# Group 0's experts on one shared tile of tokens, its rows gathered on TensorE

## The chip, the cores and the metric

One of the eight cores of one Trainium2 chip runs the whole kernel. The metric is device microseconds of one execution, lower is better. The engines are TensorE (PE; PEld is its weight load), VectorE (DVE), ScalarE (ACT), GpSimd (POOL) and SyncE (SP), which only issues DMAs here. Each engine has a queue of its own and works in program order.

## The reference

One decoder layer on 512 tokens of 1024 channels, in float32: `x1 = x + gate1 * mixer(h)`, then a hierarchical mixture of experts on `h2 = rms_norm(x1) * g + sh`, where `g` and `sh` are rows made from the condition `c`.

```
grp = softmax(h2 @ w_group + b_group); g = argmax(grp)             # one of 4 groups per token
sel = (h2 @ w_router + b_router) of group g; top 2 of its 4 experts
y   = sum over the 2 experts of  p_g * softmax(top 2) * (silu(h2 @ w_gate) * (h2 @ w_up)) @ w_down
out = x1 + gate2 * y
```

There are 16 experts in 4 groups; each has 3 MB of weights (1024x256 gate and up, 256x1024 down).

## The kernel before

The mixer runs first (to about 598 us), with `x1` as its result in two buffers, T1 (token tiles 0 and 1) and T2 (tiles 2 and 3) of 128 tokens each. Its last stage, the output projection, goes through steps (t, g) of token tile t and 256 columns g; (2,2), (2,3), (3,2), (3,3) are the last. `Weave` runs generators beside it: at each tick, those that are due emit their next piece, so the order on every engine is fixed when the program is built. `tile_chain(t)` takes the norm, logits and h2 rows of a finished tile; `h2_rows` writes the rows to a DRAM tile `h2_d`.

After (3,3) the last columns are transposed, `norm2(3)`, logits and `route(2)` give each token its group and experts, `ranks` (products with a triangular matrix) give every token its place among an expert's tokens, `one_hot(e)` makes a 128-column one-hot of the places, `slot_rows(e)` turns it into token numbers and POOL gathers the rows of `h2_d`. `busy(n)` are dummy products that keep TensorE occupied meanwhile.

The loop over `e` from 0 to 16 then works on 128 slots of one expert a turn: `gate_up` (in four parts), `act_t` (transposes the activation of the expert before), `x_rows(e + 1)` (eight transposes of gathered rows), `down(e - 1)`, with the next expert's weight splits and slots in between. Experts 0 to 3 are those of group 0, each with a tile of its own; then come eight of the two larger groups, the fullest of them a second time (index 7, by `EX`); the lightest of groups 1 to 3 shares one tile (`GL`, indices 13 to 16): one gather, one scatter, and `down` adds the four up in PSUM. `down` of a tile's last expert ends in a scatter with add to `out`. Experts with over 128 tokens besides go through a dynamic loop at the end.

Weights come as half-megabyte chunks through a ring of `NRAW` raw buffers (22), loaded by SP in an order `SEQ`; chunk j + NRAW takes the buffer of chunk j. Chunk numbers of expert e < 5: gate/up first half (0: 0, 1; 1: 2, 3; 2: 8, 9; 3: 14, 15; 4: 22, 23), down (0: 6, 7; 1: 12, 13; 2: 18, 19; 3: 24, 25). Chunks 16 and 17 use buffer T1, 18 and 19 use T2. Loads from chunk 26 on wait until chunk j - 5 has landed (`HOLD_FROM`, `AHEAD`). A new tile in a buffer waits until every access of the old tile, wherever it stands in the program, is done. A product of two float32 operands is exact enough as one native product or as three products of high and low halves (`mm3`, after `split` on ScalarE and VectorE); expert 0 is native, the second half of every gate/up too.

Of the kernel before, what the change touches and what calls it, by code (L numbers as in the profile page):

```python
# [171 lines left out]
def trunk(ctx: ExitStack, tc: tile.TileContext, I, out, dbg=None):  # L172
# [793 lines left out]
    def mod_rows(hf):  # L966
# [18 lines left out]
        for j in range(4):  # L985
# [14 lines left out]
            if hf == (j < 2):  # L1000
                A.dma_start(mod_d[1 - hf:2 - hf, 512 * (j % 2):512 * (j % 2) + 512], bm[0:1])
            yield 1

    def router_consts():
        lst = sml("lst")[:, 0:128]
        A.dma_start(lst, I["cst"][:, C_LST:C_END])
        A.dma_start(R.mcol, mod_d.rearrange("a (k p) -> p a k", p=128))
# [9 lines left out]
        V.scalar_tensor_tensor(R.mcol[:, 0], R.mcol[:, 0], 1.0, pv[:, PV_G2:PV_G2 + 8], OP.add, OP.mult)  # L1017
# [104 lines left out]
    NRAW = 2 * len(RAWS) + 2  # L1122
# [15 lines left out]
    held = []  # L1138

    def load_raw(j, hold=False, eng=SY):  # L1140
        if j >= 96:
            return
        if hold:
            held.append(j)
            return
# [6 lines left out]
        if j >= NRAW:  # L1152
            raws[j] = raws[j - NRAW]
            if j % 2 == 0:
                duo[j] = duo[j - NRAW]
        elif j % 2:
            raws[j] = raws[j - 1, 1]
        else:
            k = RAWS[j // 2] if j < 2 * len(RAWS) else "P"
            t = {"X": lambda: R.rawx.tile([128, 2048], FT, name="raw_x"),  # L1160
                 "P": lambda: R.ep.tile([128, 2048], FT, name="raw_p", bufs=1)}.get(k, lambda: big(k, "raw_e"))()
            raws[j], raws[j, 1] = t[:, 0:1024], t[:, 1024:2048]
            duo[j] = t
# [19 lines left out]
    def f():  # L1183
# [5 lines left out]
        for n, shp, dt in (("cst", [C_LST], FT), ("wrs", [8, 27], FT), ("brb", [27], FT), ("ex_i", [1], I32), ("ssp", [4, 4], FT), ("ssum", [4], FT),  # L1189
                           ("rs2", [4], FT), ("LG", [4, 27], FT), ("EL", [4, 22], FT), ("MT", [2, 4, 8], FT),   # L1190
                           ("mem", [4, 20], FR), ("lst", [128], FR), ("tok", [4, 4], FR), ("e16", [4, 16], FT), ("e4", [4, 4], FT), ("z", [2, 4], FT), ("nmem", [4, 20], FT), ("mcol", [2, 8], FT), ("PC", [20, 10], FT), ("PP", [8, 10], FT), ("PL", [4, 10], FT),
# [9 lines left out]
        R.xg = pool("xgp", wps).tile([128, 1024], FT, name="xg")  # L1201
# [31 lines left out]
    def logits(t, ks, last=7, b=None):  # L1233
# [17 lines left out]
    def norm_lg(t):  # L1251
        V.scalar_tensor_tensor(R.LG[:, t], R.LG[:, t], R.rs2[:, t:t + 1], R.brb, OP.mult, OP.add)

    def h2_gain(t, c0, n):
        c = slice(c0, c0 + n)
        G.tensor_tensor(R.xg[:, c], X1(t)[:, c], st["mod", 1][:, c], OP.mult)

    def h2_rows(t, hf, mode):
        s = slice(hf * 512, hf * 512 + 512)
        s2 = slice(1024 + hf * 512, 1024 + hf * 512 + 512)  # L1260
        h2 = sml("h2")
        rs, sh = R.rs2[:, t:t + 1], st["mod", 0][:, s2]
        if mode[0] == "V":
            V.scalar_tensor_tensor(h2, X1(t)[:, s], rs, st["mod", 1][:, s], OP.mult, OP.mult)
        elif mode == "A":
            A.activation(h2, X1(t)[:, s], AF.Copy, scale=rs)
            G.tensor_tensor(h2, h2, st["mod", 1][:, s], OP.mult)
        elif mode == "gA":
            A.activation(h2, R.xg[:, s], AF.Copy, scale=rs)
        if mode == "gV":  # L1270
            V.scalar_tensor_tensor(h2, R.xg[:, s], rs, sh, OP.mult, OP.add)
        else:

            def end(eng=G):
                eng.tensor_tensor(h2, h2, sh, OP.add)
                SY.dma_start(h2_d[t * 128:(t + 1) * 128, s], h2)
            if mode == "VV":
                return lambda: end(V)
            end()
            return  # L1280
        SY.dma_start(h2_d[t * 128:(t + 1) * 128, s], h2)
# [4 lines left out]
    def route(t0):  # L1286
# [3 lines left out]
        V.tensor_reduce(m1[:, :, 0:1], lg[:, :, 0:4], AX.X, OP.max)  # L1290
# [32 lines left out]
    def tile_chain(t):  # L1323
# [5 lines left out]
        logits(t, range(4, 8))  # L1329
        norm_lg(t)  # L1330
        if t == 1:
            route(0)
        yield 1
        h2_rows(t, 1, "A" if t < 1 else "V")
        if t < 2:
            h2_rows(t, 0, "V")
        else:
            st["h2"] = h2_rows(t, 0, "VV")

    def last_half():  # L1340
        x1_t(3, 512, 256)
        h2_gain(3, 512, 256)
        yield 1
# [21 lines left out]
    def f():  # L1365
# [3 lines left out]
        for t, g in seq:  # L1369
# [27 lines left out]
    def busy(n):  # L1397
        for _ in range(n):
            T.matmul(wb, ones_c, ones_c[:, None, :].to_broadcast([128, 4, 128]), start=True, stop=True)

    wb = bank("mm")
    lb = logits(3, (4, 5))
    busy(3)
# [5 lines left out]
    gp = pool("gp", es, bufs=5)  # L1409
# [9 lines left out]
    def w_units(w):  # L1419
# [5 lines left out]
        def gu_unit(q, i):  # L1425
# [11 lines left out]
            if q % 2:  # L1437
                load_raw(AT[w, j] + NRAW, hold="placed" not in st)
# [12 lines left out]
    def used(e):  # L1451
# [21 lines left out]
    def slot_rows(e, b=None):  # L1473
# [4 lines left out]
        idx = R.sm2.tile([128, 1], I32, name="idx", bufs=8)  # L1478
        V.tensor_copy(idx, b[:, 0:1])
        X = st["mod", 1][:, 0:1024] if e % 2 else ep.tile([128, 1024], FT, name="X", bufs=1)  # L1480
        G.indirect_dma_start(X, None, h2_d, bass.IndirectOffsetOnAxis(idx[:, 0:1], 0))
        X_[e], idx_[e] = X, idx
# [12 lines left out]
    def slots(e):  # L1495
        if e < GL:
# [4 lines left out]
        for ti in range(NT):  # L1501
            T.matmul(b[:, 0:8], oh[:, ti], R.twL[:, ti], start=ti == 0, stop=ti == 3)
# [3 lines left out]
        wsl_[GL] = w8  # L1506

    def x_rows(e):
        if e > GL:
# [29 lines left out]
    def activate(e):  # L1539
        b, act = gb.pop(e), sml("act")  # L1540
        A.activation(act[:, 0:256], b[:, 0:256], AF.Silu)
        if e < GL:
            V.tensor_tensor(act[:, 0:256], act[:, 0:256], b[:, 256:512], OP.mult)
        else:
            V.scalar_tensor_tensor(act[:, 0:256], act[:, 0:256], wsl_[GL][:, e - GL, 0:1], b[:, 256:512], OP.mult, OP.mult)
# [20 lines left out]
    def down(e, js=(0, 1)):  # L1566
        dn, aT = wfull[wset(e)][1], aT_[e]
        y = st["mod", 0][:, 1024 * (min(e, GL) % 2):1024 * (min(e, GL) % 2) + 1024]
        for j in js:
            if e <= GL:  # L1570
# [3 lines left out]
            for k in range(2):  # L1574
                s0, s1 = e <= GL and k == 0, (e < GL or e == NE - 1) and k == 1
# [5 lines left out]
            if e < GL:  # L1581
                V.scalar_tensor_tensor(y[:, c], b, wsl_[e][:, 0:1], g, OP.mult, OP.mult)  # L1582
            elif e == NE - 1:
# [4 lines left out]
        if GL <= e < NE - 1:  # L1588
            return
        e = min(e, GL)  # L1590
        G.indirect_dma_start(out, bass.IndirectOffsetOnAxis(idx_[e][:, 0:1], 0), y, None, compute_op=OP.add)  # L1591
# [3 lines left out]
    x1_t(3, 768, 256)  # L1595
    busy(3)
    norm2(3)
    st.pop("h2")()
    h2_rows(3, 0, "gV")
    out_rows(3)  # L1600
    h2_gain(3, 768, 256)
    logits(3, (6, 7), b=lb)
    norm_lg(3)
    rb, cb = bank(), bank()

    def ranks(tm):
        for tj in tm:
            for ti in range(tj, 4):
                T.matmul(rb[:, ti * 20:(ti + 1) * 20], R.lst if ti == tj else ones_c, R.mem[:, tj], start=tj == ti == 0, stop=tj == 3)
            T.matmul(cb[:, 0:20], ones_c, R.mem[:, tj], start=tj == 0, stop=tj == 3)  # L1610
    h2_rows(3, 1, "gA")
    U[0]()
    route(2)
    U[2]()
    ranks((0, 1))
    busy(10)
    ranks((2, 3))
    busy(8)
    load_raw(18)

    def flush(n):
        for j in held[:n]:
            load_raw(j, eng=A if SEQ[j][0] < PRE else SY)
        del held[:n]
# [12 lines left out]
    def lightest():  # L1637
        t3 = R.sm2.tile([128, 3], FT, name="g_t", bufs=1)
        m1 = R.sm2.tile([128, 1], FT, name="g_m", bufs=1)
        V.scalar_tensor_tensor(t3, R.PC[:, 17:20, 4], 4.0, iota(3), OP.mult, OP.add)  # L1640
        V.tensor_reduce(m1, t3, AX.X, OP.min)
        V.tensor_scalar(gs, t3, m1, None, OP.is_equal)
        V.tensor_scalar(gn, gs, -1.0, 1.0, OP.mult, OP.add)
        t = R.sm2.tile([128, 2, 4, 10], FT, name="pl_t", bufs=1)
# [5 lines left out]
        V.tensor_copy(R.perm[:, 0:8], R.PP[:, :, 9])  # L1650

    tokb = R.cst[:, C_TOK:C_TOK + 4]
    rv = rb[:, 0:80].rearrange("p (t e) -> p t e", t=4)
    V.scalar_tensor_tensor(R.pa, rv, -2.0, tokb[:, :, None].to_broadcast([128, 4, 20]), OP.mult, OP.add)
    V.tensor_tensor(R.pa, R.pa, cb[:, None, 0:20].to_broadcast([128, 4, 20]), OP.add)
    V.tensor_tensor(R.pa, R.pa, R.nmem, OP.mult)
    V.tensor_tensor(R.PC[:, :, 0:4].rearrange("p e t -> p t e"), R.pa, rv, OP.add)
    U[4]()
    one_hot(0)
    U[1]()  # L1660
    slot_rows(0)
    busy(5)
    one_hot(1)
    U[6]()
    U[3]()
    slot_rows(1)
    SY.value_load(idx_[1][0:1, 0:1])
    for j in range(19, NRAW):
        load_raw(j)
    V.tensor_copy(R.PC[:, :, 4], cb[:, 0:20])  # L1670
    one_hot(2)
    busy(12)
    weights()
# [20 lines left out]
    def overflow():  # L1694
# [52 lines left out]
    U[5]()  # L1747
    x_rows(0)
    slot_rows(2)
    lightest()  # L1750
    st["placed"] = True
    flush(9)
    U[7]()
    hi_lo(R.tw[:, 0:4, :, 1:3], R.PC[:, 0:4, 5:9])
    hi_lo(R.tw[:, 4:6, :, 1:3], R.PP[:, 0:2, 5:9])
    ov = overflow()
    DN = U[8:]
    none = [lambda: None] * 8
# [134 lines left out]
```

## Time and profile before

| | us |
|---|---|
| median of 3 runs | 805.98 (803.31 to 811.71) |
| the profiled execution | 806.46 |
| its span, first to last instruction | 804.6 |
| TensorE busy | 759.2 (94%) |
| VectorE busy | 558.0 (69%) |
| mean granted TensorE clock | 0.985 |

The span is what the instructions cover; the profiled execution's own time is 1.9 us more. Busy TensorE counts pipelined products from start to modelled end, so it can be busy without being at its peak. DMA moved 148.5 MB, 185 GB/s over the span, and 330 to 366 GB/s from 640 to 760 us.

### The profile page before, as it was taken

The page shows a single profiled execution, that of the slowest core. Times are in us where ns is not written, and L with a number is a line of the kernel's source. Part 1 is how long each engine was busy: PE and PEld are TensorE (multiplying, and loading weights), DVE is VectorE, ACT ScalarE, POOL GpSimd, SP SyncE. Part 2 cuts the span into 40 slices and gives each one's busy share as a digit, 9 for nine tenths or more (in the row PEclk, how much of TensorE's full clock was granted, in tenths as well). Part 3 has the DMA queues.
Part 4 walks back from the last instruction along what each step waited for, and adds up shares of the span by engine and source line. Part 5 has one row for each costly group of instructions (what it writes and reads, how often), then busy time and mean ns, then how long its engine had stood idle before and what let it go on. Part 6 is the DMA issues. An engine that isn't in the chain of part 4 may idle for free. (4 is left out here: it accounts for less than half of the span.)

```text
span 804.6 us, 11741 instructions
## 1 busy us (share of the span) xinstructions
PE 759.2 (94%) x4261; PEld 628.2 (78%) x4262; DVE 558.0 (69%) x1046; ACT 313.5 (39%) x556; POOL 177.8 (22%) x162
## 2 busy tenths in 40 slices
PE   7699997999999999999899999999988999999994
PEld 4477986998888899998688887889975677777662
DVE  5987737778748776775777777745476788677761
ACT  5424743242334224322344333434212454355550
POOL 2522207422121013320110031300161223221100
PEclk9799999999999999999999999999989999999998
DMA  9882243221212121358445576597556999999931
GB/s 300 255 260 90 67 129 136 77 78 59 73 53 94 64 79 53 100 190 253 139 144 163 173 229 219 163 304 234 214 185 242 321 345 363 363 363 354 331 97 27
DMA packets 68596, 148.53 MB, mean 185 GB/s; under 512 B 8189, under 2 KB 35986, under 8 KB 68282
## 3 DMA queue, kind: packets, MB, share of 16 engines
q1 hardware_dynamic: 59234, 130.00, 47.4%
q0 software_dynamic: 4032, 14.68, 7.2%
q10 hardware_dynamic: 5272, 3.09, 1.4%
q8 instruction: 34, 0.56, 0.3%
q14 instruction: 24, 0.20, 0.1%
HBM read 136.21 MB, written 12.86 MB: 185 GB/s over the span
## 5 line engine op out<-in xcount | busy, mean ns | idle before, releaser
L226 DVE TENSOR_TENSOR wlo<-raw,whi 128x1024 fp32r<-128x1024 f32 x70 | 92.2, 1321 | 60.6 <-ACT whi L225 60.5
L216 PE MATMUL bank_mm<-whi,hTh 128*128 128x256 f32 x352 | 100.9, 287 | 0.0
L216 PE MATMUL bank_mm<-wlo,hTh 128*128 128x256 f32 x352 | 98.8, 281 | 1.8 <-DVE wlo L226 1.8
L216 PE MATMUL bank_mm<-whi,hTl 128*128 128x256 f32 x352 | 98.8, 281 | 0.0
L216 PE MATMUL bank_mm<-hTh,whi 128*128 128x512 f32 x224 | 92.4, 413 | 0.0
L225 ACT ACTIVATE whi<-raw 128x1024 fp32r<-128x1024 f32 x70 | 73.2, 1054 | 48.6 <-DMA raw<-in_w_t_dram 30.5
L216 PE MATMUL bank_mm<-hTh,wlo 128*128 128x512 f32 x224 | 88.9, 397 | 0.0
L216 PE MATMUL bank_mm<-hTl,whi 128*128 128x512 f32 x224 | 88.4, 395 | 0.0
L216 PEld LDWEIGHTS bank_mm<-wlo,hTh 128*128 128x128 f32 x352 | 66.4, 189 | 2.2 <-DVE wlo L226 2.0
L216 PEld LDWEIGHTS bank_mm<-whi,hTh 128*128 128x128 f32 x352 | 66.4, 189 | 0.6 <-issue 0.3
L216 PEld LDWEIGHTS bank_mm<-whi,hTl 128*128 128x128 f32 x352 | 66.3, 188 | 0.0
L216 PE MATMUL bank_mm<-whi,mgs 128*128 128x256 f32 x256 | 51.5, 295 | 0.2 <-DVE mgs L229 0.2
L216 PEld LDWEIGHTS bank_mm<-hTh,whi 128*128 128x128 f32 x224 | 42.2, 188 | 11.0 <-issue 1.0
L216 PEld LDWEIGHTS bank_mm<-hTh,wlo 128*128 128x128 f32 x224 | 42.1, 188 | 10.6 <-DVE wlo L226 0.5
L216 PEld LDWEIGHTS bank_mm<-hTl,whi 128*128 128x128 f32 x224 | 42.1, 188 | 10.0 <-issue 0.7
L216 PE MATMUL bank_ms<-dnh,aT 128*128 128x512 f32 x120 | 45.8, 441 | 0.0
L963 DVE SCALAR_TENSOR_TENSOR acc<-raw,c_act,acc 128x1024 f32<-128x1024 f32 x28 | 37.9, 1368 | 8.3 <-DMA raw<-in_w_mod_dram 7.9
L1591 POOL DMA_INDIRECT out_dram<-modb,idx x14 | 25.2, 1797 | 81.1 <-DVEq L1875 27.1
L216 PEld LDWEIGHTS bank_mm<-whi,mgs 128*128 128x128 f32 x256 | 42.6, 199 | 0.5 <-DVE mgs L229 0.4
L216 PE MATMUL bank_mm<-wlo,mgs 128*128 128x256 f32 x128 | 37.2, 291 | 0.0
L900 POOL TENSOR_TENSOR mg<-mg,ut 128x512 f32<-128x512 f32 x8 | 11.2, 1409 | 101.3 <-DVE ut L898 101.3
L1582 DVE SCALAR_TENSOR_TENSOR modb<-bank_ms,wsl,modb 128x512 f32<-128x512 f32 x26 | 19.5, 751 | 18.3 <-PE bank_ms L216 16.3
(439 smaller groups left out, 1798.0 us busy)
## 6 DMA issues: line engine op xcount, KB each, us to landing
raw<-in_w_t_dram SPq DMA_DIRECT2D x35, 512.0 KB, 3.5
raw<-in_w_mod_dram SPq DMA_DIRECT2D x32, 512.0 KB, 4.5
raw<-in_w_m_dram SPq DMA_DIRECT2D x24, 512.0 KB, 3.2
wmod<-in_w_mod_dram SPq DMA_DIRECT2D x16, 512.0 KB, 7.4
raw_x<-in_w_ed_dram SPq DMA_DIRECT2D x16, 512.0 KB, 9.2
raw_x<-in_w_eg_dram SPq DMA_DIRECT2D x15, 512.0 KB, 9.9
raw_x<-in_w_eu_dram SPq DMA_DIRECT2D x15, 512.0 KB, 8.5
raw_e<-in_w_eg_dram SPq DMA_DIRECT2D x14, 512.0 KB, 5.9
```

The lines of the kernel that those rows point to most:

```text
L216: T.matmul(o, l[a], r[b], start=first and i == 0, stop=last and i == 2)
L225: A.activation(hi, src, AF.Copy)
L226: (eng or V).tensor_tensor(lo, src, hi.bitcast(FT), OP.subtract)
L900: G.tensor_tensor(m, m, u, OP.add)
L963: V.scalar_tensor_tensor(acc[:, c], raw, c_act[:, kt:kt + 1], acc[:, c], OP.mult, OP.add)
L1582: V.scalar_tensor_tensor(y[:, c], b, wsl_[e][:, 0:1], g, OP.mult, OP.mult)
L1591: G.indirect_dma_start(out, bass.IndirectOffsetOnAxis(idx_[e][:, 0:1], 0), y, None, compute_op=OP.add)
```

## The change

Group 0's four experts share one tile, as the lightest other group does (`shared`, `first`, `last` say which). Its rows don't come from `h2_d`: `group(t)`, `group_ranks(t)` and `group_hot(t)` make, per token tile, a one-hot of the places within group 0, scaled by the norm; `gather(t)` multiplies it with x1 into two PSUM banks, and `x_group` copies, transposes and applies gain and shift (from `mcolx`). Which group is lightest, and so the experts' order, is taken from the group sizes (`group_sums`, `lightest`) ahead of `route(2)`. `route(0)` moves from `tile_chain(1)` to step (3,2); `route(2)`, later ranks, positions and weights move into expert 0; the h2 rows of tiles 2 and 3 are written in experts 0 and 1; the gather of expert 4 is issued in expert 2. `busy` and held loads are gone. The raw ring has 26 chunks, the ring of split tiles 3 pairs in place of 5.

```diff
-    NRAW = 2 * len(RAWS) + 2
+    NRAW = 2 * len(RAWS) + 6
...
+    def group(t):
+        m1 = R.MT[:, 0, t, 0:1]
+        V.tensor_reduce(m1, R.LG[:, t, 0:4], AX.X, OP.max)
+        V.tensor_tensor(R.gm[:, t], R.LG[:, t, 0:4], m1.to_broadcast([128, 4]), OP.is_equal)
+        V.tensor_scalar(R.pen[:, t:t + 1], R.gm[:, t, 0:1].bitcast(FT), -1024.0, 1024.0, OP.mult, OP.add)
...
+    def group_hot(t):
+        p0 = R.p0[:, t:t + 1]
+        V.tensor_tensor(p0, st["rg"][:, 4 * t:4 * t + 1], R.pen[:, t:t + 1], OP.add)
+        V.tensor_scalar(st["oh0"][:, t], R.cst[:, C_IOTA:C_IOTA + 128], p0, R.rs2[:, t:t + 1], OP.is_equal, OP.mult)
+
+    def gather(t, hfs=(0, 1)):
+        if "X0" not in st:
+            st["X0"] = [bank(), bank()]
+        for hf in hfs:
+            T.matmul(st["X0"][hf], st["oh0"][:, t], X1(t)[:, 512 * hf:512 * hf + 512], start=t == 0, stop=t == 3)
...
             if (t, g) == (3, 2):
                 wv.start(last_half(), 1)
+                route(0)
+                gather(0)
...
-    gp = pool("gp", es, bufs=5)
+    gp = pool("gp", es, bufs=3)
...
+    gather(1, (0,))
+    x1_t(3, 768, 256)
+    norm2(3)
+    gather(1, (1,))
+    logits(3, (6, 7), b=lb)
+    norm_lg(3, lb)
+    group(3)
+    gather(2, (0,))
+    group_ranks(3)
+    group_hot(3)
+    gather(2, (1,))
+    group_sums()
+    gather(3)
     ranks((0, 1))
+    x_group()
+    out_rows(3)
...
+    for j in (16, 17, 20, 21, 24, 25):
+        load_raw(j)
...
     lightest()
+    for j in (22, 23):
+        load_raw(j)
+    route(2)
...
         gate_up(e, (0, 1))
         if e == 0:
-            one_hot(3)
-            flush(9)
+            x_halves()
         U[0]()
         U[1]()
-        next(ov, None)
+        if e == 0:
+            ranks((2, 3))
+            positions()
+            weights()
+            places()
+        else:
+            next(ov, None)
         gate_up(e, (2, 3))
         if e:
             act_t(e - 1)
+        if e == 0:
+            one_hot(0)
+            hi_lo(R.tw0.rearrange("p t e i -> p e t i"), R.PC[:, 0:4, 5:9])
...
+        if e == 2:
+            slots(4)
...
         gate_up(e, (6, 7))
+        if e == 0:
+            slots(0)
         activate(e)
+        if e < 2:
+            h2_rows(2 + e, 0)
+            h2_rows(2 + e, 1)
+        if e == 0:
+            for j in (18, 19):
+                load_raw(j)
```

## Rows read from the trace of the kernel before

**Rows 1.** The page's first part: busy time, share of the span, instructions.
```profile
PE 759.2 (94%) x4261; PEld 628.2 (78%) x4262; DVE 558.0 (69%) x1046; ACT 313.5 (39%) x556; POOL 177.8 (22%) x162
```
**Rows 2.** Waits of TensorE, 598 to 770 us: total, times, longest.
```profile
PE bank_ms L1519 <- DMA modb<-h_d,idx: 1.5, 1, 1.5
PE bank_ms L1609 <- DVE mem L1307: 1.0, 1, 1.0
PE bank_ms L1519 <- DMA X<-h_d,idx: 0.9, 1, 0.9
```
**Rows 3.** Stretches: length, busy time of five engines, PEclk, DMA share, GB/s.
```profile
586.00:589.00 3.00, 0.15 (x1) 0.15 (x2) 2.90 (x15) 0.11 (x1) 0.71 (x1) 1.00 0.46 175
590.00:596.50 6.50, 6.50 (x32) 6.50 (x32) 4.43 (x10) 0.89 (x3) 5.41 (x5) 0.50 0.63 199
...
660.00:680.00 20.00, 20.00 (x89) 14.31 (x88) 17.35 (x34) 10.64 (x21) 5.36 (x5) 1.00 1.04 354
```
**Rows 4.** Timeline of TensorE: start, duration in us, line, what, count, idle before.
```profile
588.85 0.44 PE L1224 MATMUL bank_ms<-ident,x 128*128 128x128 f32 x2 [3.05 <-DVE x L1216]
...
614.76 3.70 PE L1535 MATMUL bank_mm<-raw_e,XTf 128*128 128x512 f32 x8
...
625.76 0.79 PE L216 MATMUL bank_mm<-guh,XTh 128*128 128x512 f32 x1
...
632.23 3.60 PE L1577 MATMUL bank_ms<-raw_x,aF 128*128 128x512 f32 x8
...
636.98 0.80 PE L216 MATMUL bank_mm<-guh,XTh 128*128 128x512 f32 x1
...
650.89 1.06 PE L1519 MATMUL bank_ms<-ident,X 128*128 128x128 f32 x8
...
661.43 1.06 PE L1519 MATMUL bank_ms<-ident,modb 128*128 128x128 f32 x8
...
755.55 0.39 PE L1551 MATMUL bank_ms<-ident,act 128*128 128x128 f32 x2
...
764.75 0.39 PE L1551 MATMUL bank_ms<-ident,act 128*128 128x128 f32 x2
```
**Rows 5.** VectorE alone in route(2), positions, weights, lightest: length, busy, PEclk, DMA.
```profile
602.20:604.80 2.60, 2.36 (x18) 1.00 0.88 345
605.30:606.55 1.25, 1.02 (x4) 1.00 0.19 43
610.30:612.25 1.95, 1.53 (x9) 1.00 0.83 206
614.90:616.70 1.80, 1.62 (x11) 1.00 1.02 419
```
**Rows 6.** Timeline of VectorE: h2 products, the last x1 block, h2 sum, splits.
```profile
581.46 0.74 DVE L1264 SCALAR_TENSOR_TENSOR h<-x,rs,modb 128x512 f32<-128x512 f32 x1
...
598.26 0.42 DVE L1216 TENSOR_TENSOR x<-x,mx 128x256 f32<-128x256 f32 x1
...
599.34 0.68 DVE L1275 TENSOR_TENSOR h<-h,modb 128x512 f32<-128x512 f32 x1
...
617.90 1.28 DVE L226 TENSOR_TENSOR gul<-raw_x,guh 128x512 fp32r<-128x512 f32 x2
```
**Rows 7.** Waits of SP's queue, 560 to 800 us: total, times, longest.
```profile
SPq L1167 <- DVE gul L226: 13.8, 7, 9.3
SPq L1166 <- DMA raw_e<-in_w_ed_dram: 13.0, 9, 3.3
```
**Rows 8.** The page's last part: a weight load in the mixer, median to landing.
```profile
raw<-in_w_t_dram SPq DMA_DIRECT2D x35, 512.0 KB, 3.5
```
**Rows 9.** Tile X, 600 to 700 us, six gathers of rows: from issue to landing.
```profile
DMA to landing us min/median/max: 4.8/7.1/8.3
```

More of the change, by code (lines that the diff above doesn't have):

```diff
@@ L1231, in x1_t, with logits @@
             xT[t, (c0 + i) // 128] = d[:, i:i + 128]
-    def logits(t, ks, last=7, b=None):
+    def logits(t, ks, b=None):
         b = b or bank()
@@ new lines, in h2_rows, with group_ranks @@
+        V.tensor_tensor(h2, h2, st["mod", 0][:, 1024 + hf * 512:1536 + hf * 512], OP.add)
+        SY.dma_start(h2_d[t * 128:(t + 1) * 128, s], h2)
+    def group(t):
[3 more added lines that the diff above has]
+        V.tensor_scalar(R.pen[:, t:t + 1], R.gm[:, t, 0:1].bitcast(FT), -1024.0, 1024.0, OP.mult, OP.add)
+    def group_ranks(t):
+        if t == 0:
+            st["rg"] = bank()
+            st["oh0"] = sml("oh0").rearrange("p (t j) -> p t j", t=4)
+        for tj in range(t + 1):
+            T.matmul(st["rg"][:, 4 * t:4 * t + 4], R.lst if tj == t else ones_c, R.gm[:, tj], start=tj == 0, stop=tj == t)
@@ new lines, in group_sums @@
+    def group_sums():
+        for tj in range(4):
+            T.matmul(st["rg"][:, 16:20], ones_c, R.gm[:, tj], start=tj == 0, stop=tj == 3)
+    def group_hot(t):
[7 more added lines that the diff above has]
+            T.matmul(st["X0"][hf], st["oh0"][:, t], X1(t)[:, 512 * hf:512 * hf + 512], start=t == 0, stop=t == 3)
@@ L1328, in tile_chain @@
         yield 2 if t < 2 else 1
[L1329 to L1332, printed above, removed]
+        norm_lg(t, logits(t, range(4, 8)))
+        group(t)
+        yield 2 if t < 2 else 1
+        group_ranks(t)
         yield 1
-        h2_rows(t, 1, "A" if t < 1 else "V")
+        group_hot(t)
         if t < 2:
-            h2_rows(t, 0, "V")
-        else:
-            st["h2"] = h2_rows(t, 0, "VV")
+            h2_rows(t, 0)
+            yield 1
+            h2_rows(t, 1)
     def last_half():
         x1_t(3, 512, 256)
-        h2_gain(3, 512, 256)
         yield 1
@@ L1495, in slots @@
     def slots(e):
-        if e < GL:
+        if not shared(e):
             slot_rows(e, slot_w(e))
@@ L1505, in slots, with x_group, x_halves @@
         V.tensor_tensor(w8[:, :, 0], w8[:, :, 0], w8[:, :, 1], OP.add)
-        wsl_[GL] = w8
+        wsl_[e] = w8
+    def x_group():
+        X = ep.tile([128, 1024], FT, name="X", bufs=1)
+        A.activation(X[:, 0:512], st["X0"][0], AF.Copy)
+        V.tensor_copy(X[:, 512:1024], st["X0"][1])
+        XT = [ep.tile([128, 4, 128], FT, name="XTf", bufs=2) for _ in range(2)]
+        for hf in range(2):
+            b = bank()
+            for k in range(4):
+                T.transpose(b[:, k * 128:(k + 1) * 128], X[:, 4 * hf + k::8], ident)
+            for k in range(4):
+                c, g, sh = b[:, k * 128:(k + 1) * 128], R.mcolx[:, 0, 4 * hf + k:4 * hf + k + 1], R.mcolx[:, 1, 4 * hf + k:4 * hf + k + 1]
+                if k % 2:
+                    V.tensor_scalar(XT[hf][:, k], c, g, sh, OP.mult, OP.add)
+                else:
+                    A.activation(XT[hf][:, k], c, AF.Identity, bias=sh, scale=g)
+        XT_[0] = [[x] for x in XT]
+    def x_halves():
+        XT = [ep.tile([128, 4, 128], FR, name="XT" + x, bufs=2) for x in "hl"]
+        split(XT[0], XT[1], XT_[0][0][0])
+        for e in GR0[1:]:
+            XT_[e] = [XT, XT_[0][1]]
     def x_rows(e):
+        if e in GR0:
+            return
         if e > GL:
@@ L1574, in down @@
             for k in range(2):
-                s0, s1 = e <= GL and k == 0, (e < GL or e == NE - 1) and k == 1
+                s0, s1 = first(e) and k == 0, last(e) and k == 1
                 if len(dn[k]) == 1:
@@ L1587, in down @@
                 load_raw(AT[wset(e), 4 + q] + NRAW)
[L1588 to L1591, printed above, removed]
+        if last(e):
+            i = idx_[GL if e >= GL else 0 if e in GR0 else e]
+            G.indirect_dma_start(out, bass.IndirectOffsetOnAxis(i[:, 0:1], 0), y, None, compute_op=OP.add)
     U = w_units(0)
[L1595 to L1604, printed above, removed]
+    rb = bank("mm")
+    cb = rb[:, 80:100]
     def ranks(tm):
@@ L1608, in ranks @@
             for ti in range(tj, 4):
[L1609 to L1614, printed above, removed]
-    ranks((0, 1))
[L1616 to L1624, printed above, removed]
+                T.matmul(rb[:, ti * 20:(ti + 1) * 20], R.lst if ti == tj else ones_c, R.mem[:, tj], start=tj == ti == 0, stop=False)
+            T.matmul(cb, ones_c, R.mem[:, tj], start=False, stop=tj == 3)
+    gather(1, (0,))
[11 more added lines that the diff above has]
+    gather(3)
+    ranks((0, 1))
+    x_group()
+    out_rows(3)
+    for u in U:
+        u()
+    for j in (16, 17, 20, 21, 24, 25):
+        load_raw(j)
     gs, gn = R.gs[:, 0], R.gs[:, 1]
@@ L1643, in lightest, with places @@
         V.tensor_scalar(gn, gs, -1.0, 1.0, OP.mult, OP.add)
+        id8 = R.sm2.tile([128, 8], FT, name="g_i", bufs=1)
+        for i in range(2):
+            V.tensor_scalar(id8[:, 4 * i:4 * i + 4], iota(4, 8), gs[:, 2 * i:2 * i + 1], None, OP.mult)
+            V.scalar_tensor_tensor(id8[:, 4 * i:4 * i + 4], iota(4, 4 + 8 * i), gn[:, 2 * i:2 * i + 1], id8[:, 4 * i:4 * i + 4], OP.mult, OP.add)
+        V.tensor_copy(R.perm[:, 0:8], id8)
+    def places():
         t = R.sm2.tile([128, 2, 4, 10], FT, name="pl_t", bufs=1)
@@ L1649, in lightest, with positions @@
             V.scalar_tensor_tensor(R.PP[:, 4 * i:4 * i + 4], g4(1 + 2 * i), gn[:, 2 * i:2 * i + 1], t[:, i], OP.mult, OP.add)
[L1650 to L1673, printed above, removed]
+    def positions():
+        tokb = R.cst[:, C_TOK:C_TOK + 4]
+        rv = rb[:, 0:80].rearrange("p (t e) -> p t e", t=4)
+        V.scalar_tensor_tensor(R.pa, rv, -2.0, tokb[:, :, None].to_broadcast([128, 4, 20]), OP.mult, OP.add)
+        V.tensor_tensor(R.pa, R.pa, cb[:, None].to_broadcast([128, 4, 20]), OP.add)
+        V.tensor_tensor(R.pa, R.pa, R.nmem, OP.mult)
+        V.tensor_tensor(R.PC[:, :, 0:4].rearrange("p e t -> p t e"), R.pa, rv, OP.add)
+        V.tensor_copy(R.PC[:, :, 4], cb)
     def choose(tiles):
@@ L1800, in trunk @@
             U[7]()
-        if e < 1:
-            next(ov, None)
         DN = U[8:]
```

121 lines of the change are left out of this document (41 added, 80 removed).

## The prediction

> **What bounds the kernel now.** I read the page's engine shares first, then TensorE's waits and the stretches of the expert stage, then the timelines around the hand-over from mixer to experts, and last the queues. TensorE is busy 94% of the span [rows 1]. In the expert stage it is the bound: from 598 us to 770 us it waits 3.4 us in three waits [rows 2], and from 660 to 680 us it is busy throughout at full clock, while the DMA engines are full too, at 354 GB/s [rows 3]. An expert with a tile of its own takes 10.54 us there, 650.89 to 661.43, and one that shares a tile 9.20 us, 755.55 to 764.75 [rows 4]. Two places are not full: a wait of 3.05 us at 588.85, on an x1 row block behind VectorE's routing [rows 4], after which the granted clock is 0.50 for 6.5 us (the 1.2 GHz level) [rows 3], and the way from the last x1 block (598.68, [rows 6]) to the first gate-up product at 614.76 [rows 4], 16.1 us, filled with dummy products and a gather through HBM. The change works on these two places and on experts 0 to 3.
>
> **Before the last x1 block.** Routing of tiles 0 and 1 moves behind step (3,2), so the 3.05 us wait and half of the 6.5 us of slow clock go: 6.3 us. In return TensorE gets the first gather product (two native 512-column products, 1.7 us by 3.60 us for four [rows 4]) and rank products, and a new wait: group_ranks(2) needs group(2), which stands on VectorE behind routing (2.4 us [rows 5]), a one-hot (0.4), half of tile 1's h2 rows (0.7 + 0.6 [rows 6]) and the logits' norm (1.0), 5.0 us from 589.4, while TensorE has 4.1 us of work from 587.8. It waits 2.4 us, from 592 to 594.4. Bounds: nothing, and 3 us with another slow stretch. The last block is then out at 597.6, 1.1 us earlier.
>
> **To the first expert.** The norm takes 1.75 us as now, scaled logits and group one-hot 1.3, ranks 0.55, the scaled one-hot 0.6, the sums and what is left of a gather half 0.7, gather(3) 1.7 (ends at 603.9, "zero" below), the copy of X 0.9, four transposes and their evacuation 1.5: 8.7 us in place of 16.1. Gate-up of expert 0 starts at 606.3, 8.5 us earlier. The dummy products that went cost nothing.
>
> **Expert 0.** It is now VectorE's, and the terms are its pitch. From zero: copy and evacuations to 2.6 us, choice of the lightest group and expert order 1.6 (11 operations took 1.62 [rows 5]), routing of tiles 2 and 3 2.45. TensorE did two native products until 4.2 and waits for ranks((2,3)) until 6.7. Then VectorE: x_halves and two weight splits 1.8 (1.28 a pair [rows 6]), positions 1.3, weights 1.9, places 0.9 [rows 5], the one-hot and its weights 1.0. At 13.4 the last slot product can start, and expert 1 starts at 13.95, that is 617.9 against 625.76 [rows 4]: 7.9 us gained.
>
> **Expert 1** has no transposes and no slots, but a native down product in front: 9.20 + 0.8 + 0.1 = 10.1 us, where 625.76 to 636.98 was 11.2 [rows 4]. It ends at 628.0. **Expert 2**: VectorE is behind, with the rows of tiles 2 and 3 (2.55 us each), the overflow choice (4 us), two one-hots, eight splits and four down-weight halves to do between 13.4 and 33.4; the down product of expert 1 wants its low half at 30.2 and waits 3.2 us. Bounds: nothing, and 5 us. With 9.2 us and two sets of slot products this puts the transposes of expert 4 (in expert 3) at 644.8, where they are at 650.89 now: 6.1 us gained, **if their rows are there**.
>
> **The rows of expert 4.** They are not, by the code. Chunks 18 and 19 go into the buffer T2, which holds x1 of tiles 2 and 3. The change issues them in expert 0, but h2_rows(3), the last reader of that x1, now runs in expert 1. A new tile in a buffer waits for all readers of the old one, so SP's queue stands still at chunk 18 until VectorE has done that read, at 28.65, that is 632.5. In order behind it on SP are chunks 19, 26, 27, 30, 31, 34, 35, 32, 33 and only then the two stores of tile 3's h2 rows, which every gather of rows needs. That SP stands still at a load until its buffer's last reader is done is seen before (13.8 us in seven loads, 9.3 us in one, behind weight splits [rows 7]); it cost nothing, as no store of rows stood behind. Each later load also waits until the fifth chunk before it has landed (13.0 us in nine, behind one tile alone [rows 7]). A lone chunk lands in 3.5 us [rows 8] and at 419 GB/s [rows 5] the next follow 1.25 us apart: chunk 30, the fifth, lands 8.5 us after 632.5, SP may then issue 35, and the stores go out at 642. Five chunks stand before them in the queue; they land at 648.5. The gather then takes 4.8 to 8.3 us, median 7.1 [rows 9]. X is there at 655.5, and the transposes are 4.6 us later than before, after a wait of 11 us. Bounds: if the stores passed the loads, nothing (6.1 us gained); if VectorE is 3 us later and the gather slow, 9 us late.
>
> After 3.05 us idle TensorE ran 6.5 us at half clock; after 11 us I charge the same 3.3 us. Bounds: nothing and 6.
>
> The gather goes by POOL's queue, the loads by SP's, and in the trace gathers beside saturated loads took up to 8.3 us, where the first one, with little beside it, took 4.8 [rows 9]. The Trainium skill, page "DMA: Bandwidth & Descriptors", section "Queues, rings and completion order", has each DMA engine take turns between queues by packets, so that a gather needn't stand behind queued loads; by that rule I would take 4.8 us and a sum 2.3 us lower. The trace's spread leaves this open, and I keep its median.
>
> **The rest.** From expert 4 on TensorE does what it did, 10.5 us each. Three scatters, four gathers, three sets of transposes, splits and one-hots go; of the DMA time that frees, nothing is on the path, as TensorE never waits for weights now, and the SP stop takes it back (some 9 us without loads; afterwards there are 33 us until expert 4, room for some 25 chunks). Four more raw chunks cost nothing: their cover is the two split tiles that go. Three split tiles are enough in program order, since a tile comes free one product group before the split that wants it; if VectorE lags this cover is gone, at up to 1 us an expert.
>
> **Sum.** 4.6 + 3.3 = 7.9 us on the profiled 806.46 us (span 804.6 and 1.9 around it, 0.5 above the median 805.98): 814.4, I say 814.
>
> **Rivals.** (1) *Not slower: the stores are early.* If SP isn't held at chunk 18, or the stores are not behind the loads, the gather is back before 644.8, and what is left is the gain: 6.1 us, 800.4; without the wait in expert 2 as well, 797.2. The point that decides is whether h2 rows of tile 3 land before about 637. For it: no row shows this wait, only its like [rows 7]. Against it: program order on SP. Then the weights would be the next bound, as the DMA engines are full already [rows 3] and would be asked 6 us earlier.
> (2) *VectorE holds experts 0 to 2 longer.* 2.5 us of idle before ranks((2,3)) may put the clock down once more (3.05 us did, [rows 3]) and every VectorE operation could be late behind ScalarE: 2 to 5 us more, all passed on to the SP stop: 817 to 820. For it: VectorE has some 27 us of work in the first 28.65 us.
> (3) *The shared tile overflows*, and the loop at the end runs for four experts. Worked out from the reference on its inputs the groups have 68, 97, 138 and 209 tokens; group 0 fits in 128. Excluded; the loop's work would be four more experts, above 42 us.
>
> **Chances.** The SP stop as I size it, 810 to 818: 0.55. Rival 1: 0.28. Rival 2: 0.12. Others of either sign: 0.05. One per cent, about what a measurement can tell from no change, is 8.1 us: below 797.9 is faster, above 814.0 slower. The first case lies over the upper bound: 0.29 slower, 0.26 within. Rival 1 gives 0.11 faster and 0.17 within, rival 2 0.12 slower, the rest 0.03 faster and 0.02 slower: 0.14 faster, 0.43 within, 0.43 slower. For 8 in 10 the range goes from 798 to 820; the first case's own range is 810 to 818.
>
> **What would show it.** In the profile after: gate-up of expert 0 at about 606; expert 1 at 618; a wait of SP for VectorE of about 10 us at chunk 18; the last h2 stores behind ten weight loads; a wait of TensorE of about 11 us at the transposes of expert 4, and a granted clock of 0.5 behind it; 10.5 us an expert after that. I am wrong if the last h2 store goes out before 637, if TensorE waits for weights after expert 5, or if expert 1 starts after 622.

## The result, and the profile after

The changed kernel takes 831.45 us (median of 4 runs, 827.93 to 833.74), the kernel before 807.48 us beside it (4 runs, 803.31 to 811.71): ratio 1.0293, 95% interval 1.0221 to 1.0365. The sign was forecast, the size was not: 24 us in place of 8. The profiled execution took 829.4 us, span 827.7; against the 804.6 before that is 23.1 us.

TensorE's longest waits from 560 to 830 us (total, times, longest); two more are under 0.8 us. In the kernel before the longest was 3.05 us ahead of the last x1 block [rows 4] and 1.5 us from 598 us on [rows 2]:

```profile
PE bank_ms L1540 <- DMA X<-h_d,idx: 19.4, 1, 19.4
PE bank_mm L1622 <- DVE mem L1307: 4.2, 1, 4.2
PE bank_ms L216 <- DVE aT L226: 2.8, 1, 2.8
PE bank_ms L1267 <- DVE gm L1259: 2.3, 1, 2.3
```

The first is TensorE before the transposes of expert 4, whose gathered rows it wants; the second the ranks of tiles 2 and 3 in expert 0; the third a low half for the down product in expert 2; the fourth the group ranks ahead of the last x1 block. The prediction has all four places, at 11, 2.5, 3.2 and 2.4 us.

The timeline shows where they lie (start, duration, line, what, idle before); it answers to [rows 4], where expert 1 starts at 625.76 and expert 4's transposes at 650.89:

```profile
606.75 1.98 PE L1556 MATMUL bank_mm<-raw_e,XTf 128*128 128x512 f32 x4
...
612.98 0.39 PE L1622 MATMUL bank_mm<-mem,lst 128*128 128x20 f32 x1 [4.25 <-DVE mem L1307]
...
622.34 0.48 PE L216 MATMUL bank_mm<-guh,XTh 128*128 128x512 f32 x1
...
669.70 1.95 PE L1540 MATMUL bank_ms<-ident,X 128*128 128x128 f32 x8 [19.41 <-DMA X<-h_d,idx]
```

So experts 0 and 1 do start earlier than before, by 8.0 and 3.4 us, and expert 4 is 18.8 us late. The reason is on SP's queue. First its waits from 600 to 672 us, which answer to [rows 7], then its issues behind the last read of x1, a row of VectorE, and POOL's gather:

```profile
SPq L1163 <- DVE h L1251: 10.1, 1, 10.1
...
SPq L1162 <- DMA raw_e<-in_w_eg_dram: 7.8, 3, 5.5
```

```profile
635.88 0.75 DVE L1251 SCALAR_TENSOR_TENSOR h<-x,rs,modb 128x512 f32<-128x512 f32 x1
...
637.01 0.81 SPq L1163 DMA_DIRECT2D raw_e<-in_w_ed_dram  x2
638.78 0.35 SPq L1163 DMA_DIRECT2D raw_e<-in_w_eg_dram  x1
639.38 0.34 SPq L1163 DMA_DIRECT2D raw_e<-in_w_eu_dram  x1
640.04 6.41 SPq L1163 DMA_DIRECT2D raw_x<-in_w_ed_dram  x2
646.78 0.33 SPq L1163 DMA_DIRECT2D raw_x<-in_w_eg_dram  x1
649.05 0.33 SPq L1163 DMA_DIRECT2D raw_x<-in_w_eu_dram  x1
650.30 0.34 SPq L1163 DMA_DIRECT2D raw_x<-in_w_eg_dram  x1
650.95 0.33 SPq L1163 DMA_DIRECT2D raw_x<-in_w_eu_dram  x1
651.33 1.03 SPq L1253 DMA_DIRECT2D h_d<-h  x2
...
660.11 1.20 POOL L1478 DMA_INDIRECT X<-h_d,idx  x1 [60.28 <-issue]
```

SP stands 10.1 us at chunk 18 until VectorE has read x1 of tile 3; then ten loads go out, one behind the other, and only at 651.33 the two stores that expert 4's gather needs. The second of them lands 7.2 us after its issue, at about 659, the gather is issued at 660.11, and X is there at 669.7. The index was cast at 642.71 already.

The stretches (length, busy time of TensorE, weight load, VectorE, ScalarE and GpSimd, PEclk, DMA share, GB/s); the first answers to [rows 3], the second goes from the ranks in expert 0 to expert 1:

```profile
590.00:596.50 6.50, 4.22 (x33) 3.79 (x32) 6.02 (x30) 0.86 (x3) 0.55 (x1) 1.00 0.42 161
...
612.98:622.34 9.36, 9.36 (x25) 5.10 (x26) 7.12 (x27) 3.29 (x7) 0.00 (x0) 0.70 0.48 149
...
637.00:651.30 14.30, 10.45 (x33) 6.78 (x31) 10.97 (x30) 4.40 (x8) 0.00 (x0) 0.88 0.78 257
651.30:659.90 8.60, 0.00 (x0) 0.00 (x0) 1.66 (x4) 0.45 (x1) 0.00 (x0) 0.58 1.01 336
659.90:669.60 9.70, 0.00 (x0) 0.00 (x0) 0.00 (x0) 0.00 (x0) 2.17 (x2) 0.50 1.00 345
...
670.00:680.00 10.00, 10.00 (x31) 6.77 (x30) 2.18 (x6) 2.25 (x3) 0.94 (x1) 0.67 0.95 341
```

The loads behind the hold run at 257 GB/s, where I had reckoned with 419. Ahead of the last x1 block the clock stays at 1.00, where it was 0.50 before. Behind the wait of 4.2 us in expert 0 it is 0.70 over 9.36 us of full work, which costs 2.8 us. Behind the wait of 19.4 us it is 0.67 over ten microseconds in which TensorE is busy throughout: 3.3 us of work.

### The profile page after: what moved, and what is told of

Read it like the earlier page. It is cut to its first block, busy times and chain, and to the rows that moved or that the text cites. A ratio compares the mean times of both kernels' runs of the same rounds, so it can differ in the third digit from the quotient of the medians.

```text
span 827.7 us, 11594 instructions
## 1 busy us (share of the span) xinstructions
PE 760.3 (92%) x4206; PEld 623.8 (75%) x4207; DVE 557.4 (67%) x1062; ACT 311.5 (38%) x552; POOL 156.4 (19%) x145
## 5 line engine op out<-in xcount | busy, mean ns | idle before, releaser
L225 ACT ACTIVATE whi<-raw 128x1024 fp32r<-128x1024 f32 x70 | 73.2, 1054 | 48.3 <-DMA raw<-in_w_t_dram 25.1
L216 PE MATMUL bank_ms<-dnh,aT 128*128 128x512 f32 x120 | 47.5, 455 | 2.8 <-DVE aT L226 2.8
L216 PE MATMUL bank_mm<-whi,mgs 128*128 128x256 f32 x256 | 49.6, 288 | 0.4 <-DVE mgs L229 0.2
L216 PEld LDWEIGHTS bank_mm<-whi,mgs 128*128 128x128 f32 x256 | 40.8, 191 | 1.1 <-DVE mgs L229 0.7
L1612 POOL DMA_INDIRECT out_dram<-modb,idx x11 | 20.2, 1840 | 76.4 <-DVEq L1896 28.3
L1556 PE MATMUL bank_mm<-raw_e,XTf 128*128 128x512 f32 x64 | 32.7, 638 | 0.1
L216 PEld LDWEIGHTS bank_ms<-dnh,aT 128*128 128x128 f32 x120 | 23.2, 194 | 11.8 <-DVE aT L226 3.3
```

The costliest lines, as they stand in the source:

```text
L216: T.matmul(o, l[a], r[b], start=first and i == 0, stop=last and i == 2)
L225: A.activation(hi, src, AF.Copy)
L1556: T.matmul(gb[e], x[0][:, kt % 4], w[0][:, kt % 2], start=kt == 0, stop=kt == 7)
L1612: G.indirect_dma_start(out, bass.IndirectOffsetOnAxis(i[:, 0:1], 0), y, None, compute_op=OP.add)
```

## The experiments

The kernel before ran beside each group of experiments, at medians of 803 to 807 us; so times of different groups are compared by their ratios to it. A trace is of one execution, whose time can lie some microseconds from the median. Spans of single executions differ by some microseconds in the mixer already, so traces are compared from the start of the last x1 block on VectorE: "expert 1" and "expert 4" are the times from there to expert 1's first product and to expert 4's transposes, "rest" from those to the end of the span. Before: 27.5, 52.6 and 153.7 us. Changed: 24.4, 71.7 and 158.0 us.

My theory: the stores of tile 3's rows are late because SP is parked at chunk 18 and they stand behind ten loads. Rivals: the work of VectorE in experts 0 to 2, or its order, is the cost, whatever the queue does; or the weights that come late with the hold are.

**The two loads behind the rows.** Chunks 18 and 19 are issued in expert 1, behind h2_rows(3), so SP isn't parked.

```
-        if e == 0:
+        if e == 1:
             for j in (18, 19):
                 load_raw(j)
+        if e == 0:
             ...
```

> The changed kernel with chunks 18 and 19 issued in expert 1, behind the stores of tile 3's h2 rows, in place of expert 0. Theory (SP held at chunk 18 until the last x1 read, and the stores queued behind ten loads): the hold of about 10 us on SP goes, the last h2 store is issued at about 637 and has landed by 641, expert 4's gather goes at about 643 when its token numbers are there, X is back at 650, and TensorE's wait of 19.4 us at the transposes of expert 4 falls to 0 to 3 us; time 808 to 812 us, 2.4 to 2.8% under the changed kernel. Rival A (the gather is late of itself, as its token numbers are only made in expert 2): the wait stays over 10 us, time over 820. Rival B (the late weight loads cost the time): as the loads 26 to 35 also go earlier, time falls too, but TensorE's waits before had a weight tile as releaser, which they did not.

815.1 us, ratio 1.0131 (1.0078 to 1.0184). No hold; the stores go out at 636.63, the gather at 646.68. Expert 4 at 58.2, rest 157.2: 13.5 us back. I had expected the gather at 643; the index was cast at 641.15, and in the two runs below the gather follows the cast by 1.15 us. That leaves the stores: eight loads had been issued in the ten microseconds ahead of them. The trace doesn't show when they landed. A wait of 4.8 us for X is left, and the time is 3 us above what I expected.

**Both tiles' rows in expert 0,** ahead of the loads.

```
-        if e < 2:
-            h2_rows(2 + e, 0)
-            h2_rows(2 + e, 1)
+        if e == 0:
+            for t in (2, 3):
+                h2_rows(t, 0)
+                h2_rows(t, 1)
```

> The changed kernel with the h2 rows of tile 3 written in expert 0, right behind those of tile 2; chunks 18 and 19 stay behind both. Theory: SP is held 3 us longer for the rows but then goes on, the stores are ahead of all loads; X is back by 651; time 808 to 813 us. The 2.8 us of VectorE that move from expert 1 to expert 0 cost at most 2 us, at the first down product. Rival C (VectorE's backlog in experts 0 to 2 is what made the rows late): no better than 825.

807.25 us, ratio 1.0027 (1.0000 to 1.0054): moving the two calls for tile 3 takes nearly the whole loss back. Expert 4 at 53.9; the wait for X:

```profile
PE bank_ms L1540 <- DMA X<-h_d,idx: 1.2, 1, 1.2
```

**The stores by another queue,** ScalarE's, for tile 3 alone. SP's hold stays.

```
-        SY.dma_start(h2_d[t * 128:(t + 1) * 128, s], h2)
+        (A if t == 3 else SY).dma_start(h2_d[t * 128:(t + 1) * 128, s], h2)
```

> The changed kernel with the two stores of tile 3's h2 rows issued by ScalarE's queue; SP stays held at chunk 18 and its loads stay late. Theory (order behind the loads, not the hold): stores go at 636 to 637, before any held load, X is back at about 651, time 808 to 814 us, though SP's hold of 10 us is still there. Rival B (the loads that the hold delays cost the time): TensorE waits for weights, time over 820.

812.2 us, ratio 1.0091 (1.0057 to 1.0125). SP's and TensorE's waits:

```profile
SPq L1163 <- DVE h L1251: 10.0, 1, 10.0
```

```profile
PE bank_ms L1540 <- DMA X<-h_d,idx: 1.0, 1, 1.0
```

This separates the two: the hold is as long as in the changed kernel, the loads behind it go out as late (636.76 to 649.30), and TensorE waits 1.0 us for X, not 19.4, and for no weights. **The wait comes from the stores that stand behind the held loads, not from the hold by itself.** As the cause of that wait both rivals fall, since VectorE's work and its order are unchanged and the loads are as late. But some 5 us are left against the moved rows above (812.2 and 807.25, in the same group), 2.2 of them in the traces ahead of expert 4 (56.1 against 53.9). Now ScalarE's queue stands still until VectorE has made the rows, and TensorE waits in expert 2 for what ScalarE makes late (ScalarE's wait from 625 to 655 us, TensorE's from 560 to 830; 0.5 of its 2.6 us is there in the changed kernel too):

```profile
ACT dnh L225 <- DVE h L1252: 4.9, 1, 4.9
```

```profile
PE bank_ms L216 <- ACT aT L225: 2.6, 2, 2.1
```

What the other 3 us are is open.

**Something to do in the wait:** 80 products into a spare bank ahead of expert 4's transposes, for the clock's part.

```
+        if e == 3:
+            db = bank()
+            for _ in range(80):
+                T.matmul(db, ones_c, ones_c[:, None, :].to_broadcast([128, 4, 128]), start=True, stop=True)
```

> The changed kernel with 80 dummy products of 512 columns (about 17.5 us) on TensorE ahead of expert 4's transposes, in its wait of 19.4 us; the result is the same. The granted clock behind the wait stays at the upper level. Theory (7 us at half clock behind the wait cost 3.4 us): 827 to 828.5 us. Rival D (behind the wait VectorE or the weights set the pace and the clock costs nothing): 830 to 832 us.

825.8 us (819.55 to 829.07), ratio 1.0281 (1.0226 to 1.0337), against 1.0293 without them: inconclusive by the medians. In the trace, of an execution of 819.55 us, the clock stays up behind the wait and the rest is 154.5 us in place of 158.0:

```profile
650.00:660.00 10.00, 10.00 (x46) 8.29 (x45) 0.00 (x0) 0.00 (x0) 2.17 (x2) 1.00 1.01 351
660.00:670.00 10.00, 10.00 (x46) 7.33 (x45) 1.78 (x6) 2.14 (x3) 0.94 (x1) 1.00 1.01 401
```

**A longer lead for the loads.** Each load waits for the twelfth before it, not the fifth.

```
-            SY.value_load(raws[j - AHEAD][0:1, 0:1].bitcast(I32))
+            SY.value_load(raws[j - (12 if j < 36 else AHEAD)][0:1, 0:1].bitcast(I32))
```

> The changed kernel, with a load of raw data waiting for the landing of the one 12 before it in place of 5, for chunks below 36. Theory A (the stores come late because each load on the same queue waits in turn for an earlier landing): the stores issue 4 to 8 us sooner behind the hold, the rows of expert 4 come 4 to 8 us sooner, and the time is 818 to 826 us. Theory B (the bytes of the ten loads ahead have to move first, whoever waits): the stores issue sooner but land as late as in the changed kernel, TensorE's wait for X stays at 17 to 20 us, and the time is 829 to 834 us.

826.76 us, ratio 1.0245 (1.0210 to 1.0279): between the two theories, and by the intervals it can't be told from the changed kernel. The trace, of an execution of 829.36 us, tells more. SP's stores, POOL's gather, and the stretches from the hold's end to the stores, to the gather, to X:

```profile
640.47 0.81 SPq L1163 DMA_DIRECT2D raw_e<-in_w_ed_dram  x2
...
649.52 0.90 SPq L1253 DMA_DIRECT2D h_d<-h  x2
...
660.67 1.20 POOL L1478 DMA_INDIRECT X<-h_d,idx  x1 [58.20 <-issue]
```

```profile
640.50:649.50 9.00, 6.12 (x17) 3.95 (x16) 7.72 (x24) 1.06 (x1) 0.00 (x0) 0.81 0.85 298
649.50:660.50 11.00, 4.26 (x17) 2.84 (x15) 4.89 (x10) 3.79 (x7) 0.00 (x0) 0.80 0.97 361
660.50:670.50 10.00, 0.00 (x0) 0.00 (x1) 0.00 (x0) 0.00 (x0) 2.17 (x2) 0.50 0.97 320
```

The stores are issued 9.1 us behind the hold's end in place of 14.3, and the gather, which follows their landing, 20.2 behind it in place of 23.1: of 5.2 us won at the issue 2.9 stay. In both kernels about the same has been moved by then: 14.3 us at 257 GB/s and 8.6 at 336 make 6.6 MB, 9.0 at 298 and 11.0 at 361 make 6.7 MB. Ten loads of 512 KB and the two stores of 256 KB are 5.8 MB of it. By these two traces it is mainly the bytes ahead in the queue that the rows wait for; the waits between the loads cost what they leave idle, 2.9 us here.

**Routing earlier, alone.** route(2) fills the 2.6 us in which VectorE has nothing to do before gather(3) has ended; in the changed kernel it stands behind the choice of the lightest group, and TensorE waits 4.2 us for its ranks.

```
+    route(2)
     gather(3)
     ...
-    route(2)
```

> The changed kernel with route(2) alone moved to just ahead of gather(3); SP's hold at chunk 18 and the order of the rows stay. Theory: expert 1 starts 2 to 4 us sooner, the hold ends as much sooner, and so do the stores and the gather: TensorE's wait for X keeps its length of 17 to 20 us and the time falls by 2 to 5 us, to 826 to 829 us. Rival: the hold's end hangs on VectorE's work in expert 1 and not on its start, and the time stays at 830 to 833 us.

824.25 us, ratio 1.0212 (1.0174 to 1.0249); the interval overlaps the changed kernel's. In the trace, of an execution of 829.26 us, expert 1 is at 20.8 (24.4), expert 4 at 68.4 (71.7), and the wait for X is 21.0 us: the whole chain slides forward by some 3.5 us and its wait stays, as the theory has it. The wait for the ranks is gone, and the granted clock is 1.00 from 611 to 624 us.

**Both tiles' rows in expert 0, and routing earlier:** the two edits above together.

> Tile 2's and 3's rows both in expert 0 (as in a2), and route(2) moved to just ahead of gather(3), where VectorE has 2.6 us with nothing to do. Theory: what eats the 8.5 us that VectorE's shorter x1 block gives is VectorE itself in expert 0 (route(2) of 2.0 us and the XTf evacuations between the ranks of tile 2 and TensorE), so the 4.2 us wait of TensorE at the ranks falls to about 2 us or less, the 10 us of slow granted clock behind it (0.66) come to 0.9 or more, and the time is 798 to 803 us against 807 of a2. Rival: expert 0's start is bound by gather(3) and its transposes, so route(2) ahead of them only pushes them back, and the time stays at 806 to 809 us.

806.27 us, ratio 0.9987 (0.9962 to 1.0013), above what the theory gave. Expert 1 comes at 21.0 (25.4 with the rows alone), but X is waited for 4.2 us: expert 4 at 51.9, only 2.0 us sooner, and the clock falls behind the wait (rest 156.0 against 154.4). The trace is of an execution of 810.4 us.

**And expert 0's evacuations by halves:** four on ScalarE, then four on VectorE, not in turns.

```
-                if k % 2:
+                if hf:
```

> b1, and the evacuations of expert 0's transposes dealt out by halves (first half on ScalarE, second on VectorE) in place of one by one. Theory: the one-by-one deal makes each engine wait for the other (0.5 and 1.4 us on VectorE); without it the gate-up products start 1 to 2 us sooner and the time is 1 to 2 us below b1's. Rival: the four evacuations on one engine in a row take as long as the alternation (4 x 0.4 to 0.5 us), and the time is b1's within 1 us.

806.85 us (798.49 to 810.5), ratio 0.9984 (0.9949 to 1.0019): no change by the medians. In the trace VectorE's four evacuations follow each other without a wait; expert 1 comes at 18.7 and expert 4 at 48.3, but the rest is 157.3. The gather of X is issued at 637.00, the stores having been issued by 622.5; VectorE casts the index in between:

```profile
605.13 1.37 DVE L1516 TENSOR_SCALAR XTf<-bank_ms,mcolx 128x128 f32<-128x128 f32 x4 [1.32 <-PE bank_ms L1512]
...
635.87 0.15 DVE L1475 CAST idx<-bank_ms 128x1 int32<-128x1 f32 x1
...
637.00 1.20 POOL L1478 DMA_INDIRECT X<-h_d,idx  x1 [38.72 <-DMA raw_x<-in_w_eu_dram]
```

Now the index is late, not the rows: expert 4's slots stand in the middle of expert 2. It was so with both tiles' rows in expert 0 and with ScalarE's queue already (casts at 641.72 and 644.09, gathers at 642.87 and 645.24, each 1.15 us behind its cast).

**Expert 4's slots at the end of expert 1** (on top of the last):

```
-        if e == 2:
-            slots(4)
...
         if e == 0:
             slots(0)
+        if e == 1:
+            slots(4)
         activate(e)
```

> The kernel with both tiles' rows in expert 0, the early route(2) and the halves dealt out, with expert 4's slots (the products that make its index) moved from the middle of expert 2 to the end of expert 1. Theory: there the rows of expert 4 are stored by 622.5 us and only the index, which VectorE casts at 635.9 us, holds the gather at 637.0 us back; with the index some 5 us sooner, TensorE's wait for X of 2.9 us goes, and so does the slow granted clock behind it (0.50 and 0.65 over 644 to 652 us, which is 3.4 us of work); the profiled span falls by 4 to 6 us to 796 to 798 us and the time to 801 to 803 us, 0.5 to 0.8% below the kernel before. Rival: the gather is held by the engines' other traffic or the slots only move the waits of VectorE into expert 1, and the time stays at 805 to 808 us.

801.38 us, ratio 0.9951 (0.9924 to 0.9979): half a per cent faster than the kernel before, clear of no change by the interval. The gather goes at 630.52, TensorE doesn't wait for X, expert 4 is at 46.8 and the rest 155.1.

**places() behind the weights of expert 0:**

> As c1_slots4_early, and places() (four instructions on VectorE, about 1.0 us in the trace) moved behind the one-hot of expert 0 and its weights, for which TensorE waits 1.3 us at the slots of expert 0. Theory: that wait falls to 0.3 to 0.6 us and the time is 0.7 to 1 us below c1's. Rival: TensorE's wait is only moved to the split units of expert 1, which VectorE reaches no sooner, and the time is c1's within 0.5 us.

802.12 us, ratio 0.9970 (0.9947 to 0.9994): no gain. The wait at expert 0's slots falls from 1.3 to 0.5 us and the one at expert 4's slots rises from 1.7 to 3.9.

**Expert 4's slots behind the first products of expert 2,** without and with the later places():

> As c1_slots4_early, with expert 4's slots behind the first two gate-up products of expert 2 in place of ahead of its activation in expert 1. In c1 TensorE waited 1.7 us there for the one-hot and X came some 2 us before it was wanted. Theory: with 1.3 us of products ahead of it that wait goes, the gather is issued at about 631.5 us and is still hidden, and the time is 0.5 to 1.5 us below c1's: 800 to 801.5 us beside 805 to 807 of the kernel before. Rival: VectorE reaches the index only behind the splits of expert 2, X is late again by 2 to 3 us, and the time is 803 to 806 us.

> As d1_slots4_expert2, with places() behind the weights of expert 0 as in c2. In c2 the wait at the slots of expert 0 fell from 1.3 to 0.5 us and the one at expert 4's slots rose from 1.7 to 3.9 us. Theory: with those slots later the second wait doesn't come back, and the time is d1's less 0.5 to 1 us. Rival: VectorE is the bound through expert 1, so what is put off in expert 0 returns at the down product of expert 1, and the time is d1's or up to 1 us more.

799.16 us, ratio 0.9941 (0.9913 to 0.9970), and 801.03 us, ratio 0.9964 (0.9939 to 0.9990). In the first the wait of 1.7 us falls to 0.3, and 1.2 us come back at a down product; by the intervals it can't be told from the 0.9951 before it. With places() later the 0.8 us saved at expert 0's slots come back as 1.4 us at a split of expert 1 and 0.5 us more at expert 4's slots: there the order of VectorE's work only moves the wait. That VectorE is the bound there was not tested further.

## Why the prediction was wrong

The mechanism was right: each of its links is in the trace, and runs took the hold and the order behind it apart. What failed are the sizes, in two steps. From the prediction's 655.5 us for expert 4's transposes to the 669.7 measured it is 14.2 us, in these terms:

| Step of the prediction | Predicted | Measured | Miss |
|---|---|---|---|
| Last x1 block out | 597.6 | 598.4 | +0.8 |
| Expert 1 starts, from there | 20.3 | 23.9 | +3.6 |
| Hold ends, from expert 1's start | 14.6 | 14.7 | +0.1 |
| Stores issued, from the hold's end | 9.5 | 14.3 | +4.8 |
| Stores land, gather issued | 6.5 | 8.8 | +2.3 |
| Gather, issue to X | 7.0 | 9.6 | +2.6 |

**The step that failed is "The rows of expert 4"**: 9.7 of the 14.2 us are there, 7.1 of them between the hold's end and the issue of the gather. I let the loads behind the hold follow 1.25 us apart, "at 419 GB/s", a rate read from 1.8 us of VectorE's own stretch [rows 5], and let SP wait once more, at chunk 35 until chunk 30 has landed. A nearer row was the stage's mean of 354 GB/s [rows 3], but the same working with it gives some 18 us for what I had at 16 and what took 23.1; so the rate that I picked is only 2 of the 7.1 us. The rest is that behind the hold, on an idle queue and in a chain of landings, the loads ran below either rate, at 257 GB/s, and none of the rows shows such a stretch. From 637 to 652 us SP waited twice for a landing, at chunk 31 for chunk 26 and at chunk 35 for chunk 30:

```profile
SPq L1162 <- DMA raw_e<-in_w_eg_dram: 5.5, 1, 5.5
SPq L1162 <- DMA raw_x<-in_w_ed_dram: 1.6, 1, 1.6
```

Chunk 26, the third in line, landed some 9 us behind the hold's end, where my pitch gives 6.0, and then the DMA engines had little to do, by their share of 0.26:

```profile
646.00:647.00 1.00, 1.00 (x4) 0.40 (x3) 0.20 (x1) 0.00 (x0) 0.00 (x0) 1.00 0.26 107
```

With the longer lead 2.9 of the 7.1 us went; what keeps the rest below 354 GB/s is open. The gather I took at the median of before, 7.1 us; the three of this tile from 600 to 700 us took 7.5 to 9.5 by the trace:

```profile
DMA to landing us min/median/max: 7.5/8.1/9.5
```

By the rule of the Trainium skill ("DMA: Bandwidth & Descriptors", "Queues, rings and completion order") that each DMA engine takes turns between the queues, the prediction would have taken 4.8 us for this gather. The trace doesn't bear that time out: it took 9.6 us beside loads at 345 GB/s.

**"Expert 0" failed by 3.6 us**, 1.6 ahead of the ranks and 2.1 behind them. I wrote that VectorE would be done with the evacuation at 606.5; it was at 609.4, since it and ScalarE waited in turn for each other:

```profile
607.18 0.81 ACT L1518 ACTIVATE XTf<-bank_ms,mcolx 128x128 f32<-128x128 f32 x2 [0.48 <-DVE XTf L1516]
...
608.96 0.41 DVE L1516 TENSOR_SCALAR XTf<-bank_ms,mcolx 128x128 f32<-128x128 f32 x1 [0.53 <-ACT XTf L1518]
```

So the wait for the ranks was 4.2 us and not 2.5. Behind it I had VectorE as the bound, but TensorE was busy throughout until expert 1, at a granted clock of 0.70: 2.8 us, which I had charged to rival 2 only. So that rival came true in part, on top of the first case, and so did a sign of being wrong that I had named: expert 1 started after 622, at 622.34. With routing moved forward expert 1 came at 20.8 us from the x1 block's start, with the halves at 18.7.

Two sums of the prediction are slightly off: the terms ahead of the first expert make 9.0 us and not 8.7, and those of expert 0 up to the last slot product 13.55 and not 13.4. Neither explains the miss.

**What held:** the waits ahead of the last x1 block (2.3, predicted 2.4) and in expert 2 (2.8, predicted 3.2); the hold (10.1, "about 10"); the charge for the clock, 3.3 us predicted and 3.3 in the stretch behind the wait (the rest of the span is 4.3 us longer than before; 0.7 of it is a wait of slot products for VectorE's low half of expert 4's activation, which the runs without the long wait have as well); and that the four chunks more and the split tiles cost nothing, as TensorE waits for no raw weights behind expert 5. Rival 1's price, 800.4 with the stores early, is 0.992 of the 806.46 and was not reached by that alone: the moved rows gave 1.003. By the runs that followed, VectorE's lag in expert 0 and then the index stood in its place; with those two mended as well 0.994 to 0.997 was measured.

My bound for this step, 9 us later than before, was the second mistake: it was built from "VectorE 3 us later and the gather slow" and had no bound for the loads' rate, the term with the largest spread between rows (419 against 354 and the single load's 3.5 us for 512 KB, which is 150 GB/s).

## What to carry to other kernels

A load that must wait for a reader parks everything behind it on its queue: before moving one up, list what is issued behind it and who wants that, and put small transfers with a consumer (rows, indices) ahead of the held load. Another queue helps as well, but its engine then stands still until the data is made, as ScalarE did for 4.9 us here. Size such a delay by the bytes ahead of the transfer, at a rate measured behind a like stop (257 GB/s here, 354 in the full stage), with a bound for that rate too. And when a wait is removed, look for the next operand of the same instruction: here first the rows, then the index was late.

## What the runs showed of the hardware

In two traces stores of 256 KB took about twice as long behind loads on their own queue as ahead of them. The DMA issues of the changed kernel from 636 to 672 us, behind ten loads (count, KB each, median from issue to landing):

```profile
h_d<-h SPq DMA_DIRECT2D x2, 256.0 KB, 7.2
```

and of the kernel with expert 4's slots at the end of expert 1, from 610 to 655 us, where the four stores of both tiles go out ahead of the held loads:

```profile
h_d<-h SPq DMA_DIRECT2D x4, 256.0 KB, 3.8
```

And the length of a wait said little of the price behind it. After 19.4 us TensorE lost 3.3 us of work to the clock, after 4.2 us in expert 0 2.8 us, after 3.05 us in the kernel before 3.25 us (0.50 over 6.5 us, [rows 3]), and after 2.3 us ahead of the last x1 block nothing (1.00 from 590 to 596.5 us).
